# Delta rule: the running inverse of the triangles' substitution in PSUM, and PSUM's banks dealt anew for the projections

## The chip, the cores and the metric

One core of a Trainium2 chip runs the whole program as one launch. The metric is the device time of one execution in microseconds (us); lower is better. The chip's matrix engine is TensorE (PE; its weight loads are listed apart as PEld), the others are VectorE (DVE), ScalarE (ACT), GpSimd (POOL) and SyncE (SP, which here only issues transfers). Each engine works off its own instructions in a fixed order. SBUF is the on-chip memory, and PSUM is the memory that TensorE writes to: here 8 banks, each 128 partitions x 512 fp32 numbers.

## The reference, cut to what matters

Two layers of a hybrid block over 768 tokens (256 of context, 512 latent), model width 1024: attention heads and a gated delta rule (8 heads of width 64, forward and backward) side by side, then a mixture of experts. The delta rule is computed in chunks of 64 tokens, and each chunk needs the inverse of a 64x64 unit lower triangle:

```python
lower = jnp.where(strict, jnp.einsum("bhnid,bhnjd->bhnij", kb, kc) * decay, 0.0)
eye = jnp.eye(CHUNK, dtype=f32)                    # CHUNK = 64
tmat = lax.linalg.triangular_solve(lower + eye, jnp.broadcast_to(eye, lower.shape),
                                   left_side=True, lower=True, unit_diagonal=True)
u = jnp.einsum("bhnij,bhnje->bhnie", tmat, vc * bc)
w = jnp.einsum("bhnij,bhnjd->bhnid", tmat, kb * jnp.exp(gcum)[..., None])
```

## The kernel before, in words

A layer runs: modulation and norm of the input; the **projections** (the stretch that the change touches); attention and the delta rule's 12 steps, interleaved; the output projection; routing and experts. All weights of the projections are split into a high and a low part, so each product is three matmuls (`mm3`, L239): high x high, high x low, low x high.

In the projections the program goes through a written list, `ORDER`, one for each layer. Its items are: `c0` to `c11`, 128 channels each (a weight split, matmuls into the PSUM tile `pt`, an evacuation to `xin` by ScalarE, a five-tap convolution on VectorE, L518); `S`, the gates' scalars; `n256`, `n512`, `n2304`, units of 256 columns of the attention and gate projections (matmuls into `pn`, evacuated by ScalarE to `gev`); and for each of three batches of chunks `i`, `s` and `m`:
- `i` (`delta_intra`): the triangles `u` of a batch, from `kk` (key products, through ScalarE) and `dd` (decays, L790 to L798), and the off-diagonal blocks `uo`. The 32x32 diagonal blocks go to memory (`db`).
- `s` (`delta_subst`): the **substitution**. The 128 partitions hold one 32x32 unit triangle each (`sB`), and `sY` its inverse. 31 steps, two VectorE instructions each: L824 multiplies a column of B with the row of Y that is done into `sT`, and L825 subtracts `sT` from the rows below. Step j works on (31-j)(j+1) numbers of each partition, 31 to 256. Each instruction needs the one before it. At the end `sY` goes to memory (`dy`, L826).
- `m` (`merge_batch`, `delta_merge`): loads `dy` as `yl`, transposes it to `yt`, and joins the 32x32 inverses to 64x64 ones with small matmuls: a pass of L847 into PSUM, a copy `mg` by ScalarE (L848), a pass of L851, a copy into `xm` (L852), twice for each direction d; then `xm` goes to memory (`xad`, L854). There is one `xm` and one `mg`, and one `yl`.

A tile scheduler decides from dependences, priorities and free buffers in which order the items of the list reach each engine, so the items overlap. Behind the list come attention (`kv_stacks` with `kt` L572, `attn_queries` with `qt` L589, the scores `sc` L604) and the delta steps, which load the merged inverses as `lx` (from `xad`) and begin with `pz` (L917).

PSUM is one pool of three kinds of buffers: "a" (`psA`: `pt`, `pn` and others, 512 columns), "c" (`psC`: `kk`, `gb`, `vt`, `kt`, `nps`, a part of the merges), "s" (`psS`, 1024 columns). Before, there are 3 + 3 + one of two banks for the whole program. When the pool is opened again with other numbers, the tiles of the new one wait for the old ones that lie in the same banks.

Of the kernel before, what the change touches and what calls it, by code (L numbers as in the profile page):

```python
# [13 lines left out]
F32 = mybir.dt.float32  # L14
# [3 lines left out]
AF = mybir.ActivationFunctionType  # L18
# [5 lines left out]
P = 128  # L24
# [80 lines left out]
UO = 10  # L105
VR = 1
SB = 2
YB = 2
RQ = 30
FW = ("gpsimd", "gpsimd")  # L110
PSA = (3, 3)
AB = 4
AHEAD = 2
XT = 3
# [7 lines left out]
XM = 1  # L122
DDB = 2
FINP = (8, 9, 10, 11)
MPS = ((0, 1), (0, 1, 2))
ORDER = ("c4 c5 c6 c7 S i0 s0 i1 s1 i2 s2 c0 c1 c2 c3 Q n256 n0 x n512 m0 m1 c8 c10 c11 c9 n2304 m2",
         "c4 c5 c6 c7 S c0 i0 s0 i1 s1 c9 i2 s2 c1 c2 c3 Q n256 n0 x n512 m0 m1 c8 c10 n2304 c11 m2")
WP = 3
# [8 lines left out]
PAIRS = ((0, 1), (2, 5), (3, 4))  # L137
# [7 lines left out]
class Model:  # L145
    def __init__(self, ctx, tc, t):
        self.tc, self.nc, self.t = tc, tc.nc, t
        self.cp = ctx.enter_context(tc.tile_pool(name="const", bufs=1, side=L))
        self.pst = ctx.enter_context(ExitStack())
        self.psum(*PSA)  # L150
        self.dr = ctx.enter_context(tc.tile_pool(name="dr", bufs=1, space=DRAM))
# [48 lines left out]

    def psS(self, name):
        return self.ps.tile([P, 1024], F32, tag="s", bufs=self.ns, name=name)

    def rsq(self, pool, a, name, newton=False):

# [606 lines left out]
    def delta_subst(self, b, db, dy, pool):  # L812

        nc = self.nc
        B = pool.tile([P, 32, 32], F32, tag="sB", bufs=SB, name="sB")
        self.q("ild").dma_start(B, db.rearrange("h q j i -> (h q) j i"))
        Y = pool.tile([P, 32, 32], F32, tag="sY", bufs=YB, name="sY")
        nc.gpsimd.memset(Y, 0.0)
        nc.gpsimd.memset(Y.rearrange("p a b -> p (a b)")[:, 0:1024:33], 1.0)
        for j in range(31):  # L820
            m, w = 31 - j, j + 1
            T = pool.tile([P, 256], F32, tag="sT%d" % (b % ST), bufs=1, name="sT")
            T3 = T[:, :m * w].rearrange("p (a b) -> p a b", a=m)
            nc.vector.tensor_tensor(T3, B[:, j, j + 1:32][:, :, None].to_broadcast([P, m, w]), Y[:, j, 0:w][:, None, :].to_broadcast([P, m, w]), op=OP.mult)  # L824
            nc.vector.tensor_tensor(Y[:, j + 1:32, 0:w], Y[:, j + 1:32, 0:w], T3, op=OP.subtract)  # L825
        self.q("iy").dma_start(dy.rearrange("h q r c -> (h q) r c"), Y)  # L826

    def delta_merge(self, tts, d, dy, us, xad, ps, pool):

# [168 lines left out]
                n = 4 * (2 * d + j)  # L998
                self.delta_intra(tt, d, kk[j], sc, us[tt, d], xad, db[:, n:n + 4], pool)

    def merge_batch(self, i, b, us, xad, dy, pool):
        ps = self.psS("mg") if b in MPS[i] else None
        for d in range(2):
            self.delta_merge(PAIRS[b], d, dy[:, 8 * d:8 * d + 8], us, xad, ps[:, 512 * d:512 * d + 512] if ps is not None else self.psC("mg"), pool)


    def gate(self, mp, ps, n, dst):
# [515 lines left out]
    def layer(self, i, xsrc, rows, done, xstack, mod):  # L1523

        nc, tc, t = self.nc, self.tc, self.t
# [8 lines left out]
        vk, xad, qkd = dr("vk", [NT, P, 2, 512]), dr("xad", [NT, 2, P, 2, 512]), dr("qkd", [NT, P, 512])  # L1534
        db = [dr("db%d_" % b, [NH, 16, 32, 32]) for b in range(3)]
        dy = [dr("dy%d_" % b, [NH, 16, 32, 32]) for b in range(3)]
# [7 lines left out]
        with self.pool("hp", B) as hp:  # L1544
            with self.pool("pj", B) as wp:
                mp.update(self.rope_params(i, wp))
                first = []
                with self.pool("nm", B) as pool:
                    start = lambda: first.extend(self.wnat(i, 2560, 288, wp))
                    hh, hl = self.norm_first(rows, start, pool, hp) if i == 0 else self.norm_mix(i, rows, start, mod, pool, hp)  # L1550
                done()
                mid = left.enter_context(self.pool("mid", A))
                ba = scl.tile([P, NT, 32], F32, name="ba", tag="ba")
                dT = [mid.tile([P, 3088], F32, name="dT%d" % j, tag="dT%d" % j).rearrange("p (a b) -> p a b", a=4) for j in range(2)]

                def nat_unit(c0, n, pool):
                    ws = first if c0 == 2560 else self.wnat(i, c0, n, wp)
                    g = pool.tile([P, NT * UNIT], F32, tag="gev", bufs=GV, name="gev").rearrange("p (t n) -> p t n", t=NT)

                    def ev(tt, ps):  # L1560
                        if c0 < 768:
                            nc.scalar.activation(g[:, tt], ps[:, :UNIT], AF.Copy)  # L1562
                        elif need(tt):
                            self.gate(mp, ps, UNIT, g[:, tt])
                        if n > UNIT:
                            nc.scalar.activation(ba[:, tt, :], ps[:, UNIT:UNIT + 32], AF.Copy)

                    f0 = 0 if c0 in (512, 2560) else t0
                    self.proj_nat(hh, hl, ws, n, range(f0, NT), ev)
                    if c0 < 512:  # L1570
                        self.qk_unit(mp, 0, g, 4, t0, pool)
                        self.q("qg").dma_start(qd[:, t0:, c0:c0 + UNIT], g[:, t0:])
                    elif c0 == 512:
                        self.qk_unit(mp, 1, g, 2, 0, pool)
                        self.q("qg").dma_start(qd[:, :, c0:c0 + UNIT], g)
                    else:
                        self.q("qg").dma_start(gd[:, t0:, c0 - 2304:c0 - 2304 + UNIT], g[:, t0:])

                def conv(f, dst, pool):
                    return self.proj_conv(i, hh, hl, self.wpart(i, 0, 8, 768 + f * P, P, wp), mp["cw"], f, dst, pool)  # L1580

                def key_conv(f, ss, pool):
                    x = dT[f // 4][:, f % 4, :]
                    self.squares(f, x, ss, conv(f, x, pool))
                    if f >= 4:
                        self.token_rows(x, None, vk[:, :, 1, (f - 4) * P:(f - 3) * P], pool)

                def value_conv(f, pool):
                    v = pool.tile([P, NT * UNIT], F32, tag="gev", bufs=GV, name="vf")[:, :772]
                    conv(f, v, pool)  # L1590
                    self.token_rows(v, sc["nk"][:, :, 2 * f - 16:2 * f - 14], vk[:, :, 0, (f - 8) * P:(f - 7) * P], pool)

                with self.pool("pp", B) as pool, self.pool("q1", A) as p1:
                    nat_unit(2560, 288, pool)

                    def query_norms():
                        sc["fq"] = scl.tile([P, NT, NH], F32, name="fq", tag="fq")
                        nc.vector.tensor_scalar(sc["fq"], self.inv_norm(ss, p1)[1], HD ** -0.5, None, op0=OP.mult)

                    us = {}  # L1600
                    for op in ORDER[i].split():
                        kind, arg = op[0], op[1:]
                        if kind == "S":
                            sc = self.delta_scalars(mp, ba, ss, scl, p1)
                        elif kind == "Q":
                            query_norms()
                        elif kind == "c":
                            f = int(arg)
                            if f in (0, 4):
                                ss = self.psS("ss")  # L1610
                            value_conv(f, pool) if f >= 8 else key_conv(f, ss, pool)
                        elif kind == "i":
                            self.intra_batch(int(arg), us, dT, sc, xad, db[int(arg)], p1)
                        elif kind == "s":
                            self.delta_subst(int(arg), db[int(arg)], dy[int(arg)], p1)
                        elif kind == "m":
                            self.merge_batch(i, int(arg), us, xad, dy[int(arg)], p1)
                        elif kind == "x":
                            for tt in range(t0, NT):
                                self.q("qk").dma_start(qkd[tt], self.delta_kk(tt, 0, dT, p1))  # L1620
                        elif kind == "n":
                            nat_unit(int(arg), UNIT, pool)
        o = left.enter_context(self.pool("oo", A)).tile([P, NT, 512], F32, name="o", tag="o")
        wrp = left.enter_context(self.pool("wr", A))
        raws = []
        with self.pool("at", B) as pool:
            st = self.kv_stacks(qd, pool)
            work = ([(pr, 0, 2, 2) for pr in range(4)] if not last else []) + [(pr, 2, 4, 6) for pr in range(4)]
# [161 lines left out]
```

## Time and profile before

| | |
|---|---|
| time, 3 runs | median 2094.74 us (2092.64 to 2094.93) |
| the profiled execution | 2092.51 us, of which the profile's span is 2090.7 us |
| mean granted clock of TensorE | 0.902 of full speed |
| busy: PE / DVE / ACT / POOL | 1763.9 us (84%) / 1460.2 (70%) / 1016.6 (49%) / 868.6 (42%) |
| projections of layer 0 | about 59 to 341 us of the span |
| projections of layer 1 | about 1145 to 1421 us |

The two stretches of projections are 27% of the span. "Busy" is the sum of an engine's instruction times; an engine can be waiting while it counts as busy, where an instruction is held up inside.

### The profile page before, as it was taken

What the parts mean: (1) busy time and instruction counts of PE and PEld (TensorE: products, weight loads), DVE (VectorE), ACT (ScalarE), POOL (GpSimd) and SP (SyncE); (2) the same over time, 40 slices, a digit from 0 to 9 for tenths busy, and PEclk for the clock granted to TensorE, in tenths of its full rate; (3) what the DMA queues carried; (4) which work ended last, traced back from release to release, by engine and by line L of the source; (5) the groups of instructions that cost most, each with busy time, mean ns of one, the idle gap of its engine ahead of it and who ended that gap; (6) DMA issues with size and microseconds to landing.
All of it is one profiled execution on the core that took longest, in us unless ns stands there. A gap on an engine that the chain in (4) does not pass through costs nothing. (4 is left out here: it accounts for less than half of the span.)

```text
span 2090.7 us, 35600 instructions
## 1 busy us (share of the span) xinstructions
PE 1763.9 (84%) x13835; PEld 1382.1 (66%) x13835; DVE 1460.2 (70%) x2472; ACT 1016.6 (49%) x1595; POOL 868.6 (42%) x915
## 2 busy tenths in 40 slices
PE   6998798978877879999996987776898577999994
PEld 4887687766656746666665866675676465777773
DVE  4469996567673668887874579992678465787774
ACT  3444344665541246565554543343566225666663
POOL 4456653234354423343226466650234443334321
PEclk9999897799998979999997998875899788999997
DMA  9222445798645389998853323445983558988872
GB/s 283 74 71 82 129 119 166 218 259 246 205 125 144 147 327 336 332 322 301 324 161 119 97 73 97 131 130 158 282 233 83 148 214 315 346 334 330 328 295 102
DMA packets 227687, 427.81 MB, mean 205 GB/s; under 512 B 83720, under 2 KB 157180, under 8 KB 202939
## 3 DMA queue, kind: packets, MB, share of 16 engines
q1 hardware_dynamic: 171547, 329.09, 47.1%
q0 software_dynamic: 33536, 72.59, 12.2%
q10 hardware_dynamic: 22432, 23.81, 3.3%
q8 instruction: 111, 1.82, 0.4%
q14 instruction: 61, 0.50, 0.1%
HBM read 386.82 MB, written 84.67 MB: 226 GB/s over the span
## 5 line engine op out<-in xcount | busy, mean ns | idle before, releaser
L1418 POOL DMA_INDIRECT yd<-ey,idx x64 | 114.2, 1784 | 425.3 <-DMA yd<-ey,idx 151.8
L1364 PE MATMUL pab<-w,xt 128*128 128x512 f32 x512 | 230.3, 592 | 0.0
L1332 ACT ACTIVATE w2h<-w 128x2048 fp32r<-128x2048 f32 x64 | 122.7, 1917 | 134.5 <-PE py L1406 83.3
L1333 DVE TENSOR_TENSOR w2l<-w,w2h 128x2048 fp32r<-128x2048 f32 x64 | 146.8, 2294 | 53.5 <-ACT w2h L1332 52.9
L1333 DVE TENSOR_TENSOR w13l<-w,w13h 128x2048 fp32r<-128x2048 f32 x64 | 146.5, 2288 | 28.9 <-ACT w13h L1332 28.9
L1364 PEld LDWEIGHTS pab<-w,xt 128*128 128x128 f32 x512 | 93.0, 191 | 92.0 <-issue 91.8
L489 POOL TENSOR_TENSOR wlo<-wraw,whi 128x1024 fp32r<-128x1024 f32 (+1 forms) x44 | 111.1, 2529 | 93.1 <-ACT whi L488 93.1
L239 PE MATMUL pn<-whi,hh 128*128 128x256 f32 (+1 forms) x432 | 134.6, 314 | 16.3 <-ACT gev L1562 12.5
L239 PE MATMUL po<-woh,m 128*128 128x512 f32 x320 | 114.1, 434 | 30.7 <-ACT woh L1069 14.5
L239 PE MATMUL pn<-whi,hl 128*128 128x256 f32 (+1 forms) x432 | 135.3, 316 | 2.0 <-DVE hl L350 1.7
L239 PE MATMUL pn<-wlo,hh 128*128 128x256 f32 (+1 forms) x432 | 132.4, 308 | 1.2 <-POOL wlo L489 1.2
L1332 ACT ACTIVATE w13h<-w 128x2048 fp32r<-128x2048 f32 x64 | 121.8, 1902 | 6.4 <-DMA w<-w 4.1
L239 PE MATMUL pt<-hh,wlo 128*128 128x512 f32 (+1 forms) x352 | 124.2, 353 | 0.0
L239 PE MATMUL pt<-hh,whi 128*128 128x512 f32 (+1 forms) x352 | 122.9, 349 | 0.0
L239 PE MATMUL pt<-hl,whi 128*128 128x512 f32 (+1 forms) x352 | 122.2, 347 | 0.0
L1406 PE MATMUL py<-w2h,gh 128*128 128x512 f32 x256 | 109.1, 426 | 4.6 <-DVE ey L1413 4.4
L1337 POOL DMA_INDIRECT xe<-h2d,idx x64 | 85.9, 1343 | 61.2 <-issue 22.9
L518 DVE SCALAR_TENSOR_TENSOR dT<-xin,cw,dT 128x772 f32<-128x772 f32 x64 | 80.1, 1252 | 43.3 <-ACT dT L516 41.5
L1406 PE MATMUL py<-w2h,gl 128*128 128x512 f32 x256 | 103.1, 403 | 7.8 <-DVE gl L1385 7.8
L1413 DVE TENSOR_TENSOR ey<-py,eg 128x1024 f32<-128x1024 f32 x64 | 78.2, 1222 | 44.1 <-PE py L1406 37.8
L239 PEld LDWEIGHTS pn<-whi,hh 128*128 128x128 f32 x432 | 90.6, 211 | 23.2 <-ACT gev L1562 13.5
L1348 PEld LDWEIGHTS xt<-cst,xe 128*128 128x128 f32 x512 | 68.3, 192 | 55.1 <-issue 29.8
(401 smaller groups left out, 5124.4 us busy)
## 6 DMA issues: line engine op xcount, KB each, us to landing
w<-w SPq DMA_DIRECT2D x192, 1024.0 KB, 9.8
araw<-ada_w POOLq DMA_DIRECT2D x40, 1024.0 KB, 6.8
wraw<-w_in SPq DMA_DIRECT2D x40, 512.0 KB, 4.1
lk<-vk SPq DMA_DIRECT2D x48, 256.0 KB, 7.2
lx<-xad SPq DMA_DIRECT2D x40, 256.0 KB, 10.0
araw<-ada_w SPq DMA_DIRECT2D x8, 1024.0 KB, 10.9
wr<-w_out SPq DMA_DIRECT2D x8, 1024.0 KB, 13.4
vk<-vr ACTq DMA_DIRECT2D x16, 384.0 KB, 3.7
```

Of the source, the lines that this page charges most:

```text
L239: self.nc.tensor.matmul(ps, a(k), b(k), start=(first and n == 0), stop=(last and n == 3 * nk - 1))
L489: getattr(nc, eng).tensor_tensor(lo, raw, hi, op=OP.subtract)
L518: nc.vector.scalar_tensor_tensor(dst, xin[:, tap:tap + 772], cw[:, tap, f:f + 1], dst, op0=OP.mult, op1=OP.add)
L1332: self.pin(nc.scalar.activation(hi, src, AF.Copy))
L1333: self.pin(nc.vector.tensor_tensor(lo, src, hi, op=OP.subtract))
L1337: self.pin(self.nc.gpsimd.indirect_dma_start(out=xe, out_offset=None, in_=h2d, in_offset=bass.IndirectOffsetOnAxis(ap=idx, axis=0), bounds ...
L1348: pin(nc.tensor.transpose(ps[:, k * P:(k + 1) * P], xe.rearrange("p (q k) -> p k q", k=8)[:, 4 * q + k, :], self.ident))
L1364: self.pin(self.nc.tensor.matmul(out, xt[:, k, :], w13[:, :, KS + k, :], start=False, stop=(k == 3)))
L1406: pin(self.nc.tensor.matmul(py[:, n * 512:(n + 1) * 512], a[:, j, :], b[:, c], start=(j + m == 0), stop=(j == 1 and m == 2)))
L1413: pin(nc.vector.tensor_tensor(y, py, gates, op=OP.mult))
L1418: self.pin(self.nc.gpsimd.indirect_dma_start(out=yd, out_offset=bass.IndirectOffsetOnAxis(ap=idx, axis=0), in_=y, in_offset=None, bounds_c ...
```

## The change

The inverse Y of a substitution moves from SBUF (`sY`) to PSUM: to the one "s" buffer, as tile `sP`. The two GpSimd fills of `sY` (L818, L819) go; ScalarE now fills `sP` with zeros (a Copy with scale 0, 128x1024) and VectorE sets the diagonal. The 31 steps are the same instructions on the same shapes, with Y in PSUM in place of SBUF. At the end ScalarE copies `sP` to `sY` in SBUF (now one buffer, before two), and `sY` goes to memory as before. Since `sP` has one buffer, a substitution can't begin before the one ahead of it has been copied out.

For the room, PSUM has two layouts. During the projections "a" has 2 banks in place of 3, "c" has 3, "s" one of two banks, and a new kind "q" (`psQ`) has one bank: it takes the merges (`mg`) and the squares' sums (`ss`), which were in "s" and "c". The layout is switched behind the norm and back ahead of attention, twice in each layer.

```diff
-YB = 2
+YB = 1
...
-PSA = (3, 3)
+PSA, PSB = (3, 3), (2, 3)
...
-MPS = ((0, 1), (0, 1, 2))
...
+    def psQ(self, name):
+        return self.ps.tile([P, 512], F32, tag="q", bufs=1, name=name)
...
         self.q("ild").dma_start(B, db.rearrange("h q j i -> (h q) j i"))
-        Y = pool.tile([P, 32, 32], F32, tag="sY", bufs=YB, name="sY")
-        nc.gpsimd.memset(Y, 0.0)
-        nc.gpsimd.memset(Y.rearrange("p a b -> p (a b)")[:, 0:1024:33], 1.0)
+        ps = self.psS("sP")
+        Y = ps.rearrange("p (a b) -> p a b", a=32)
+        nc.scalar.activation(ps, self.cst[:, :1024], AF.Copy, scale=0.0)
+        nc.vector.memset(ps[:, 0:1024:33], 1.0)
         for j in range(31):
...
-        self.q("iy").dma_start(dy.rearrange("h q r c -> (h q) r c"), Y)
+        res = pool.tile([P, 32, 32], F32, tag="sY", bufs=YB, name="sY")
+        nc.scalar.activation(res, Y, AF.Copy)
+        self.q("iy").dma_start(dy.rearrange("h q r c -> (h q) r c"), res)
...
-    def merge_batch(self, i, b, us, xad, dy, pool):
-        ps = self.psS("mg") if b in MPS[i] else None
+    def merge_batch(self, b, us, xad, dy, pool):
         for d in range(2):
-            self.delta_merge(PAIRS[b], d, dy[:, 8 * d:8 * d + 8], us, xad, ps[:, 512 * d:512 * d + 512] if ps is not None else self.psC("mg"), pool)
+            self.delta_merge(PAIRS[b], d, dy[:, 8 * d:8 * d + 8], us, xad, self.psQ("mg"), pool)
...
                 done()
+                self.psum(*PSB)
...
-                                ss = self.psS("ss")
+                                ss = self.psQ("ss")
...
+        self.psum(*PSA)
         with self.pool("at", B) as pool:
```

The lines behind the edits move down by 2 to 5 in the changed kernel (L239 is L241 there, L824 and L825 are L827 and L828). In the rows below a number behind a name tells tiles of one name apart.

**Place 1: TensorE at the end of the norm, layer 1.** `nps` are the norm's transposes, `pn` the matmuls of the first unit of the projections. Before, they alternate:

```order
L343 MATMUL nps<-cst,x_11014 128x128
L239 MATMUL pn<-whi,hl 128x288
L239 MATMUL pn<-whi,hh 128x288
L239 MATMUL pn<-wlo,hh 128x288
L239 MATMUL pn<-whi,hl 128x288
L343 MATMUL nps<-cst,x_11012 128x128
L343 MATMUL nps<-cst,x_11014 128x128
L239 MATMUL pn<-whi,hh 128x288
```

Now the unit stands behind all of the norm:

```order
L345 MATMUL nps<-cst,x_11028 128x128
L345 MATMUL nps<-cst,x_11030 128x128
L345 MATMUL nps<-cst,x_11028 128x128
L345 MATMUL nps<-cst,x_11030 128x128
L241 MATMUL pn<-whi,hh 128x288
L241 MATMUL pn<-wlo,hh 128x288
L241 MATMUL pn<-whi,hl 128x288
```

Of the unit's 144 matmuls, 72 (layer 0) and 108 (layer 1) stood ahead of the norm's last transpose; now none does, in either layer.

**Place 2: VectorE at the turn from substitution 0 to 1, layer 0.** Before, the two are interleaved, with other work between (`ud` is of `delta_intra`):

```order
L824 TENSOR_TENSOR sT_1308<-sB_1264,sY_1266 128x252
L824 TENSOR_TENSOR sT_1486<-sB_1481,sY_1483 128x31
L825 TENSOR_TENSOR sY_1266<-sY_1266,sT_1308 128x18x14
L825 TENSOR_TENSOR sY_1483<-sY_1483,sT_1486 128x31
L824 TENSOR_TENSOR sT_1311<-sB_1264,sY_1266 128x255
L805 SCALAR_TENSOR_TENSOR ud_1636<-u_1632,cst_63,ud_1636 128x256
L824 TENSOR_TENSOR sT_1489<-sB_1481,sY_1483 128x60
L825 TENSOR_TENSOR sY_1266<-sY_1266,sT_1311 128x17x15
```

Now they follow each other, with the last steps of one, three instructions of an attention unit, and the first step of the next:

```order
L827 TENSOR_TENSOR sT_1363<-sB_1268,sP_1270 128x31
L828 TENSOR_TENSOR sP_1270<-sP_1270,sT_1363 128x31
L538 TENSOR_REDUCE qss_2537<-qsq_2535 128x8
L540 TENSOR_SCALAR qss_2537<-qss_2537 128x8
L822 MEMSET sP_1489 128x32
L542 TENSOR_TENSOR gev_2352<-gev_2352,qr_2540 128x512
L827 TENSOR_TENSOR sT_1492<-sB_1487,sP_1489 128x31
```

In layer 1 the MEMSET stands directly behind the last step at both turns. Over the program's 372 such instructions, 121 stood directly behind the one of the same substitution that they need; now 231 do.

**Place 3: TensorE at the end of the projections, layer 0.** `pn` is the last unit, `mg` the last merges, `kt`, `qt` and `sc` attention. Before, attention stands among the merges:

```order
L239 MATMUL pn<-whi,hl 128x256
L847 MATMUL mg<-yt,uo 32x32 x32
L851 MATMUL mg<-yl,mg 32x32 x16
L572 MATMUL kt<-cst,xl 128x128 x6
L589 MATMUL qt<-cst,ql 128x128 x2
L851 MATMUL mg<-yl,mg 32x32 x16
L604 MATMUL sc<-ka,qs 128x256
```

Now all merges come first:

```order
L241 MATMUL pn<-whi,hl 128x256
L852 MATMUL mg<-yt,uo 32x32 x16
L856 MATMUL mg<-yl,mg 32x32 x32
L852 MATMUL mg<-yl,uo 32x32 x32
L856 MATMUL mg<-yt,mg 32x32 x32
L852 MATMUL mg<-yt,uo 32x32 x32
L856 MATMUL mg<-yl,mg 32x32 x32
L574 MATMUL kt<-cst,xl 128x128 x6
L591 MATMUL qt<-cst,ql 128x128 x2
L606 MATMUL sc<-ka,qs 128x256
L606 MATMUL sc<-kb,qs 128x256
L922 MATMUL pz<-lk,lx 64x64
```

In layer 1 `kt` and `qt` stood ahead of the last batch's merges, and now stand behind them.

## Rows read from the trace of the kernel before

**Rows 1.** Windows: busy PE, PEld, DVE, ACT, POOL; clock; DMA share; GB/s

```profile
165.00:342.00 177.00, 150.82 (x1487) 134.59 (x1487) 167.32 (x330) 69.51 (x134) 99.10 (x90) 0.91 0.38 106
342.00:393.00 51.00, 41.94 (x459) 35.71 (x459) 20.38 (x56) 34.09 (x82) 10.25 (x13) 0.53 0.59 180
1260.00:1421.50 161.50, 121.35 (x1180) 106.57 (x1180) 150.01 (x319) 61.18 (x118) 99.46 (x81) 0.82 0.45 128
```

**Rows 2.** Timeline, ends of the projections: start, length, instruction, [idle before <-releaser]

```profile
338.44 0.19 DVE L825 TENSOR_TENSOR sY<-sY,sT 128x31 f32<-128x31 f32 x1
341.41 0.28 PE L239 MATMUL pn<-whi,hl 128*128 128x256 f32 x1
...
393.27 0.47 PE L917 MATMUL pz<-lk,lx 64*64 64x64 f32 x2
...
1421.03 0.19 DVE L825 TENSOR_TENSOR sY<-sY,sT 128x31 f32<-128x31 f32 x1
...
1451.78 1.91 PE L851 MATMUL mg<-yl,mg 32*32 32x32 f32 x32 [0.74 <-ACT xm L852]
...
1461.24 0.45 PE L917 MATMUL pz<-lk,lx 64*64 64x64 f32 x2 [0.23 <-DMA lx<-xad]
```

**Rows 3.** Windows, VectorE busy in L824 alone, then in L825

```profile
165.00:342.00 177.00, 44.95 (x93) 0.91 0.38 106
1260.00:1421.50 161.50, 42.46 (x93) 0.82 0.45 128
...
165.00:342.00 177.00, 42.67 (x93) 0.91 0.38 106
1260.00:1421.50 161.50, 38.71 (x93) 0.82 0.45 128
```

**Rows 4.** Timeline of VectorE, two neighbouring steps in layer 1

```profile
1396.53 0.42 DVE L824 TENSOR_TENSOR sT<-sB,sY 128x252 f32<-128x252 f32 x1
1396.98 0.42 DVE L825 TENSOR_TENSOR sY<-sY,sT 128x252 f32<-128x252 f32 x1
```

**Rows 5.** Timeline of VectorE and of GpSimd, the same moment in layer 0

```profile
303.02 0.41 DVE L824 TENSOR_TENSOR sT<-sB,sY 128x252 f32<-128x252 f32 x1
303.34 1.02 DVE L518 SCALAR_TENSOR_TENSOR vf<-xin,cw,vf 128x772 f32<-128x772 f32 x1
...
305.54 2.62 DVE L824 TENSOR_TENSOR sT<-sB,sY 128x255 f32<-128x255 f32 x1
...
304.74 3.14 POOL L489 TENSOR_TENSOR wlo<-wraw,whi 128x1024 fp32r<-128x1024 f32 x1 [6.36 <-ACT whi L488]
```

**Rows 6.** Instructions of two lines: ns min/median/max; first and last start; shapes

```profile
L793 DVE TENSOR_TENSOR dd<-gb,gcum x24: 643/678/693, 135.2 to 1321.6; 128x512 f32<-128x512 f32 x24
L798 DVE TENSOR_TENSOR u<-kks,dd x24: 676/685/2884, 148.3 to 1331.9; 128x512 f32<-128x512 f32 x24
```

**Rows 7.** The same view: two more lines

```profile
L326 ACT ACTIVATE sq<-x x12: 1009/1027/1029, 17.4 to 1126.6; 128x1024 f32<-128x1024 f32 x12
L347 DVE TENSOR_SCALAR nT<-nps,fm x18: 527/536/545, 25.0 to 59.3; 128x256 f32<-128x256 f32 x18
```

**Rows 8.** Timeline of TensorE behind layer 1's norm; `pn` back to back

```profile
1146.18 0.30 PE L239 MATMUL pn<-whi,hh 128*128 128x288 f32 x1
1146.31 0.30 PE L239 MATMUL pn<-wlo,hh 128*128 128x288 f32 x1
```

**Rows 9.** What TensorE waited for, 60 to 342 us: total, times, longest

```profile
PE kk L778 <- ACT kks L781: 7.5, 3, 5.0
PE kk L778 <- DVE dd L793: 7.3, 2, 3.7
PE pn L239 <- ACT gev L1562: 5.9, 1, 5.9
PE pn L239 <- ACT ba L1566: 3.1, 1, 3.1
```

**Rows 10.** The same for ScalarE

```profile
ACT uo L802 <- DVE u L798: 30.0, 9, 5.1
```

More of the change, by code (lines that the diff above doesn't have):

```diff
@@ L1616, in layer @@
                         elif kind == "m":
-                            self.merge_batch(i, int(arg), us, xad, dy[int(arg)], p1)
+                            self.merge_batch(int(arg), us, xad, dy[int(arg)], p1)
                         elif kind == "x":
```

## Prediction

> **What bounds the kernel now.** I first cut the span into stretches and read each engine's busy time, then looked at where the two stretches of projections end, then at the substitution's own instructions. In [rows 1] the reader is to see that VectorE is the engine that sets the second half of the projections: in layer 0, 167.3 of 177 us busy against 150.8 of TensorE, so TensorE stands idle for 26 us; in layer 1, 150.0 of 161.5 against 121.4, with 40 us idle and a granted clock of 0.82. Behind it comes a stretch with little work at half clock (0.53). The chain that matters is in [rows 2]: the last subtraction of substitution 2 ends at 338.6 and 1421.2 us, then come the merges, and the delta steps begin (`pz`) at 393.3 and 1461.2. In layer 0 TensorE's last projection ends 3 us after the substitution, so both engines end together there; in layer 1 the substitution alone is last.
>
> Now the substitution itself. By [rows 3] its 186 instructions in a layer take 44.95 + 42.67 = 87.6 us in layer 0 and 42.46 + 38.71 = 81.2 in layer 1, half of VectorE's time. What would they take undisturbed? The shortest form, 31 numbers, takes 0.19 us [rows 2], and 252 numbers take 0.42 [rows 4]: 1.04 ns for a number, and 0.16 fixed. The 31 steps have 5456 numbers, twice: 62 x 0.15 + 10912 x 0.00104 = 20.7 us for a substitution, 62 for a layer. So 25 us in layer 0 and 19 in layer 1 are excess. Where it comes from is in [rows 5]: a 255-number multiplication takes 2.62 us, and GpSimd begins `wlo`, from SBUF to SBUF, in the same stretch; it lasts 3.14. [Rows 6] show the same on a pair of lines with equal shape: L798, both operands in SBUF, ranges from 676 to 2884 ns; L793, one operand in PSUM, never takes more than 693 in 24 times. In PSUM, Y makes both instructions of a step like L793.
>
> **The change part by part.**
>
> The collisions: −25 and −19 us of VectorE, if [rows 6] carry over. They hold for a PSUM operand that is read. L827 only reads one; L828 also writes to PSUM, and no row shows a VectorE instruction that does. Bounds: the dearest PSUM operand is L347, 0.536 us for 256 numbers [rows 7] against 0.42, so +0.12 on the 186 writes, 22 us in all; below, L793's 678 against L798's 685, nothing. I take nothing, since L793 is the nearest row: same operation, same engine, a two-operand form.
>
> The steps follow each other closer. 110 more instructions stand directly behind the one that they need (231 against 121). Such a neighbour begins 0.03 us after the end of the other (1396.98 − 1396.53 = 0.45 at a length of 0.42 [rows 4]); an independent one begins 0.09 before it (303.34 against 303.02 + 0.41 [rows 5]). 110 x 0.12 = 13 us, 6.5 a layer.
>
> The turns between substitutions. The one `sP` is copied out by ScalarE, zeroed by ScalarE, and given its diagonal, before the next can begin. A Square of 128x1024 into PSUM takes 1.03 us [rows 7]; I take that for fill and for copy, with 0.2 for the MEMSET and some 0.3 for the hand-overs: 2.5 us. Where other VectorE work stands between, it is covered: by the order one turn of layer 0 and none of layer 1, so 2.5 and 5 us. The first fill and the GpSimd fills that go cost and bring nothing: no one waits for them.
>
> So VectorE's part is −25 + 6.5 + 2.5 = −16 in layer 0, and −19 + 6.5 + 5 = −7 in layer 1, where `kt` and `qt` also go behind the merges, and take their VectorE work out of the stretch; I count −2 for that, what is left when they are done later at a better clock.
>
> The switch of the layout. TensorE no longer puts the first unit into the gaps of the norm. 72 and 108 matmuls that lay beside the norm now follow it, at 0.13 us each by [rows 8] (I count 0.136, with the gaps between groups): 10 and 15 us. Against it: the norm ends a little sooner without them, 2 to 3 us, and in layer 0 the 3.1 us wait for `ba` [rows 9] no longer comes in the same way. I take +5 and +12. The bounds are 0 (if VectorE's chain behind it had room) and 25 in all.
>
> Two banks "a" in place of three. A tile has 24 matmuls, 2.9 us at 256 columns (0.136 x 256/288 = 0.12). TensorE can be one tile less ahead of ScalarE, so a late evacuation costs up to a tile. Below: the two places where three banks ran out already, `gev` 5.9 and `ba` 3.1 us [rows 9], 6 us in all. Above: ScalarE itself stands 9 times behind VectorE's `u` [rows 10], up to 5.1 us, and each would cost a tile, 26 us. I take 6, since TensorE waits for an evacuation only in those two rows; most of ScalarE's idle time is not on a `pt`.
>
> The end of the projections, layer 0. Substitution 2 ends at 338.6 − 16 + 5 = 328. TensorE: of its 26 idle us some 14 were waits for `kks` and `dd` (7.5 + 7.3 [rows 9]), which follow VectorE; 341.7 − 14 + 5 + 3 = 336. The merges then run with nothing between, from the end of the last unit: in layer 1 the like of it took from 1421.2 to 1453.7, 32.5 us [rows 2], with passes of 1.91 + 0.74. So 368; `xad` and its loads 7 us, as from 1453.7 to 1461.2: `pz` at 375, 18 sooner. But the attention that stood among the merges is now behind them. In the 51 us from 342 TensorE was busy for 41.9 at a clock of 0.53 [rows 1]; some 12 passes of the merges, 1.91 each [rows 2], are 23 of it, and the other 19 are attention, 10 us at full clock, less what fits in the 7 us of loads: +8. Layer 0: −10, with bounds −18 (the attention hides) and 0.
>
> Layer 1: +12 −7 −2, one more ScalarE copy ahead of `dy`, +1, and 3 for the banks' lower bound, which leaves +5 after 2 us of the switch's loss have gone into waits for `dd`. The sum: −10 + 5 = −5 us. Against the profiled execution, 2092.5: 2087.5; the median lies 2.2 higher, so I forecast **2089.7**, say 2090.
>
> **The rivals.**
>
> Bigger gain: TensorE follows VectorE fully. For: 40 idle us and a clock of 0.82 in layer 1 [rows 1]; at 0.95 its 121 us would be 105. With layer 0 at its bound, −18, and layer 1 at −8, −26: 2069. Against: the idle time has several releasers, and the switch takes place ahead of it.
>
> Nothing to see: VectorE's gain is real but the switch's lower cost in TensorE's order, 10 + 15 us, takes all of it. It needs only 5 us more than I count: 2095.
>
> Two banks decide, and the kernel gets slower. The place is the stretch of `c` items with `i` between, where ScalarE waits for `u` and can't empty `pt`. The price is 2.9 us each time; from 4 such tiles beyond the two that I count the change loses, and with all nine it is 20 us more: 2110. For: 30 us of such waits [rows 10]. Against: TensorE's list of waits has hardly a `pt` in it.
>
> PSUM itself costs: each instruction with Y in PSUM is dearer by a fixed time, as L347 is by 0.12 us [rows 7]. On the 186 writes that is 22 us, of which some 18 reach the end: 2108; on all 372, 2130. [...]
>
> **How the numbers follow.** The forecast's own range is 2080 to 2099: layer 0's bounds, and 5 either way for switch and banks. Chances: the forecast 0.42, the bigger gain 0.15, nothing to see 0.12, two banks 0.17, PSUM itself 0.09, something else 0.05 (slower). The range from 2068 to 2110 takes in the bigger gain and the two banks and leaves out the far end of PSUM itself and of the rest. A run of this kernel can tell some 0.2%, 4.2 us, from no change: faster is below 2090.5, slower above 2098.9. Of the forecast's 0.42, 0.25 lies below and 0.15 within, 0.02 above; so faster 0.42, same 0.27, slower 0.31.
>
> **What would show it.** Right: L827 and L828 in two windows at 62 to 65 us a layer with no single one above 0.6 us, whatever GpSimd does; neighbours 0.03 us apart; a gap of 2 to 3 us at the turns of layer 1; `pn` beginning behind the last `nps`; `pz` near 375 us in layer 0 and near 1466 in layer 1 less what layer 0 gave. Wrong: L828's shortest form at 0.25 us or more (PSUM itself), TensorE waits for `xin` or `gev` of 15 us and more in a layer (two banks), or long instructions still among L827 and L828, which would put their cause elsewhere than at the shared reads.

## The result, and the profile after

The changed kernel takes **2122.3 us** (median, 2122.09 to 2132.77 in 4 runs) against 2094.84 of the kernel before in the same comparison: ratio 1.0143, 95% interval 1.0117 to 1.0169. It is slower by 27.5 us; the forecast was 2090 (2068 to 2110).

The substitution did what was forecast. Its two lines in the changed kernel, as instructions of a line (ns min/median/max, first and last start):

```profile
L827 DVE TENSOR_TENSOR sT<-sB,sP x186: 173/353/422, 190.7 to 1453.4; 128x31 f32<-128x31 f32 x12, 128x60 f32<-128x60 f32 x12, 128x87 f32<-128x87 f32 x12, 128x112 f32<-128x112 f32 x12
L828 DVE TENSOR_TENSOR sP<-sP,sT x186: 180/366/432, 192.0 to 1453.6; 128x31 f32<-128x31 f32 x12, 128x60 f32<-128x60 f32 x12, 128x87 f32<-128x87 f32 x12, 128x112 f32<-128x112 f32 x12
```

The windows of L827, then of L828, as [rows 3]:

```profile
165.00:342.00 177.00, 30.80 (x93) 0.91 0.45 131
1300.00:1460.00 160.00, 30.96 (x93) 0.77 0.48 139
...
165.00:342.00 177.00, 32.05 (x93) 0.91 0.45 131
1300.00:1460.00 160.00, 31.99 (x93) 0.77 0.48 139
```

No instruction is above 0.432 us, where before one of 2.62 stood beside GpSimd's `wlo` [rows 5]. A layer's 186 instructions take 62.9 us, against 87.6 and 81.2 [rows 3]. The ends of the stretches, on the timelines of VectorE and TensorE, as [rows 2]; the last three rows are the end of attention in layer 0 and layer 1's first `pz`:

```profile
337.42 0.20 DVE L828 TENSOR_TENSOR sP<-sP,sT 128x31 f32<-128x31 f32 x1
...
328.08 0.28 PE L241 MATMUL pn<-whi,hl 128*128 128x256 f32 x1
370.20 1.91 PE L856 MATMUL mg<-yl,mg 32*32 32x32 f32 x32 [0.74 <-ACT xm L857]
372.05 1.86 PE L574 MATMUL kt<-cst,xl 128*128 128x128 f32 x6
378.62 0.45 PE L922 MATMUL pz<-lk,lx 64*64 64x64 f32 x2 [0.48 <-DMA lx<-xad]
...
609.22 0.33 PE L903 MATMUL pq<-S,dT 64*64 64x64 f32 x4
635.24 0.39 PE L647 MATMUL pv<-pl,vs 128*128 128x512 f32 x1
...
1487.27 0.32 PE L922 MATMUL pz<-lk,lx 64*64 64x64 f32 x2
```

Up to layer 0's first `pz` the change is ahead: 378.6 against 393.3 [rows 2]. The lead is not where the forecast had it: the last subtraction ends at 337.6, only 1 us sooner than before, but TensorE's last projection ends at 328.4, 13 us sooner, and the last merge is done 34.5 us behind the substitution, where it was 47 before (at 386.0).

But attention's last value (`pv`) comes at 635.2, 26 us behind the last delta step (`pq`, 609.2). In the kernel before the last values start at 599.7, among the last delta steps (its last `pq` starts at 601.5). Values of layer 0 before (two halves), then after:

```profile
L645 PE MATMUL pv<-ph,vs x64: 280/398/628, 365.3 to 599.5; 128*128 128x512 f32 x48, 128*128 128x256 f32 x16
L645 PE MATMUL pv<-pl,vs x64: 279/394/628, 366.1 to 599.7; 128*128 128x512 f32 x48, 128*128 128x256 f32 x16
```

```profile
L647 PE MATMUL pv<-ph,vs x64: 279/393/793, 385.2 to 635.0; 128*128 128x512 f32 x48, 128*128 128x256 f32 x16
L647 PE MATMUL pv<-pl,vs x64: 278/398/795, 386.4 to 635.2; 128*128 128x512 f32 x48, 128*128 128x256 f32 x16
```

So from `pz` to the last value layer 0 takes 257 us in place of 207. Layer 1's first instruction on TensorE (`cw`) comes at 1132.1 in place of 1104.2: 27.9 of the 29.8 us that lie between the two profiled executions. From there to its first `pz` layer 1 takes 355.2 us against 357.0.

What attention's tail looks like, on TensorE's timeline of the changed kernel and then ScalarE's:

```profile
616.39 1.54 PE L628 MATMUL ptr<-cst,pp 128*128 128x128 f32 x6 [3.39 <-ACT pp L620]
622.17 1.54 PE L628 MATMUL ptr<-cst,pp 128*128 128x128 f32 x6 [4.24 <-ACT pp L620]
625.90 0.79 PE L647 MATMUL pv<-ph,vs 128*128 128x512 f32 x1 [2.19 <-ACT ph L639]
```

```profile
618.36 2.94 ACT L1073 ACTIVATE woh<-wr 128x1024 fp32r<-128x1024 f32 x3
621.20 0.92 ACT L620 ACTIVATE pp<-pp,sm 128x768 f32<-128x768 f32 x1
622.02 2.94 ACT L1073 ACTIVATE woh<-wr 128x1024 fp32r<-128x1024 f32 x3
```

With no delta step left to fill the gaps, TensorE waits 2 to 4 us at links of the chain score, maximum, exponential, scale (`pp`), transpose (`ptr`), `ph`, value; and on ScalarE the links queue behind the output projection's weight splits `woh`, three at a time, 2.9 us.

### The profile page after: what moved, and what is told of

It reads as the page before. It is cut to its first block, busy times and chain, and to the rows that moved or that the text cites. A ratio compares the mean times of both kernels' runs of the same rounds, so it can differ in the third digit from the quotient of the medians.

```text
span 2120.5 us, 35611 instructions
## 1 busy us (share of the span) xinstructions
PE 1777.8 (84%) x13835; PEld 1384.9 (65%) x13835; DVE 1421.8 (67%) x2478; ACT 1028.1 (48%) x1607; POOL 840.2 (40%) x903
## 5 line engine op out<-in xcount | busy, mean ns | idle before, releaser
L1422 POOL DMA_INDIRECT yd<-ey,idx x64 | 120.2, 1878 | 417.4 <-DMA yd<-ey,idx 161.0
L241 PE MATMUL pn<-whi,hh 128*128 128x256 f32 (+1 forms) x432 | 132.3, 307 | 5.1 <-ACT gev L1567 3.0
L241 PE MATMUL po<-woh,m 128*128 128x512 f32 x320 | 111.0, 424 | 27.9 <-ACT m L1045 15.6
L241 PE MATMUL pn<-wlo,hh 128*128 128x256 f32 (+1 forms) x432 | 130.7, 303 | 3.1 <-POOL wlo L491 3.1
L241 PE MATMUL pn<-whi,hl 128*128 128x256 f32 (+1 forms) x432 | 130.5, 302 | 0.0
L241 PE MATMUL pt<-hh,wlo 128*128 128x512 f32 (+1 forms) x352 | 123.4, 351 | 0.0
L241 PE MATMUL pt<-hh,whi 128*128 128x512 f32 (+1 forms) x352 | 122.0, 347 | 0.0
L241 PE MATMUL pt<-hl,whi 128*128 128x512 f32 (+1 forms) x352 | 121.7, 346 | 0.0
L1352 PEld LDWEIGHTS xt<-cst,xe 128*128 128x128 f32 x512 | 68.2, 192 | 58.5 <-issue 29.8
L1366 PE MATMUL pab<-w13h,xth 128*128 128x512 f32 x256 | 103.0, 403 | 0.5 <-ACT xth L1354 0.5
```

The costliest lines, as they stand in the source:

```text
L241: self.nc.tensor.matmul(ps, a(k), b(k), start=(first and n == 0), stop=(last and n == 3 * nk - 1))
L1352: pin(nc.tensor.transpose(ps[:, k * P:(k + 1) * P], xe.rearrange("p (q k) -> p k q", k=8)[:, 4 * q + k, :], self.ident))
L1366: self.pin(self.nc.tensor.matmul(out, a[:, k, :], b[:, :, k, :], start=(k + m == 0), stop=False))
L1422: self.pin(self.nc.gpsimd.indirect_dma_start(out=yd, out_offset=bass.IndirectOffsetOnAxis(ap=idx, axis=0), in_=y, in_offset=None, bounds_c ...
```

## The experiments

Each was timed beside the kernel before, whose median was 2094 to 2096 us in each of the comparisons. The marks below are from the profiled execution: the start of the first `pz` and the end of the last `pv` of layer 0, the start of layer 1 (`cw`), and the time from there to layer 1's first `pz`.

| kernel | pz, layer 0 | last pv, layer 0 | layer 1 starts | to its pz | time, median | ratio to before (95%) |
|---|---|---|---|---|---|---|
| before | 393.3 | 600.1 | 1104.2 | 357.0 | 2094.8 | 1 |
| changed | 378.6 | 635.6 | 1132.1 | 355.2 | 2122.3 | 1.0143 (1.0117 to 1.0169) |
| e1 gate | 383.2 | 631.8 | 1118.4 | 358.0 | 2116.3 | 1.0108 (1.0063 to 1.0152) |
| e2 late | 383.3 | 613.8 | 1109.4 | 374.1 | 2119.8 | 1.0124 (1.0080 to 1.0169) |
| e3 layout | 388.5 | 651.9 | 1140.1 | 363.5 | 2146.7 | 1.0267 (1.0213 to 1.0321) |
| e4 sub | 402.8 | 660.7 | 1153.8 | 360.1 | 2148.2 | 1.0257 (1.0212 to 1.0301) |
| e5 l0 | 387.6 | 626.0 | 1120.0 | 357.3 | 2105.1 | 1.0055 (1.0031 to 1.0079) |
| e6 l0q | 378.2 | 616.8 | 1110.5 | 357.3 | 2111.2 | 1.0096 (1.0064 to 1.0127) |
| e7 early | 377.1 | 618.1 | 1108.3 | 350.6 | 2094.0 | 0.9997 (0.9971 to 1.0023) |
| e8 norm | 396.9 | 624.0 | 1127.5 | 371.3 | 2131.0 | 1.0182 (1.0138 to 1.0225) |
| e9 norm, order | 397.0 | 606.0 | 1106.8 | 375.5 | 2111.8 | 1.0102 (1.0066 to 1.0138) |
| e10 after, order | 403.8 | 609.2 | 1110.7 | 358.5 | 2106.8 | 1.0073 (1.0038 to 1.0108) |
| e11 best | 381.3 | 601.3 | 1101.9 | 354.8 | 2092.3 | 0.9989 (0.9968 to 1.0010) |
| e12 best, Y in SBUF | 399.9 | 621.2 | 1120.9 | 365.6 | 2118.4 | 1.0130 (1.0103 to 1.0157) |

Each mark is of a single execution, and it scatters. In layer 0, e2 and e5 have the same instructions, on each engine in the same order but for a few neighbours that changed places; yet their last values come 12 us apart, and layer 1 starts at 1109.4 in one and at 1120.0 in the other. (e2's profile is of a run of 2111.9 us, where the median is 2119.8; e5's of one of 2112.0, where it is 2105.1.) So some 10 us between two marks show nothing by themselves; the times have to agree. The values of layer 0 in e2, then in e5:

```profile
L647 PE MATMUL pv<-ph,vs x64: 279/396/797, 352.0 to 612.7; 128*128 128x512 f32 x48, 128*128 128x256 f32 x16
L647 PE MATMUL pv<-ph,vs x64: 281/398/795, 357.0 to 625.0; 128*128 128x512 f32 x48, 128*128 128x256 f32 x16
```

**First round: where is the loss?** Theory A: the switch ahead of attention. Theory B: the projections, by two banks or by PSUM as such.

e1, on the kernel before:

```diff
         raws = []
+        self.psum(*PSA)
         with self.pool("at", B) as pool:
```

> The kernel before, with PSUM's pool opened anew (same 3, 3 and one) ahead of attention and nothing else. Theory A (the switch back ahead of attention is the loss: attention waits for the last merge and has no head start over the delta steps): in layer 0 two scores instead of 24 ahead of step 0, an attention tail of 20 to 35 us behind the last delta step, 2115 to 2130 us in all; the substitution is untouched. Theory B (the loss is in the projections: two banks, or PSUM as such): no switch of numbers, Y in SBUF, so 2090 to 2100.

Theory A holds: with Y and the layout untouched, opening the pool anew puts all merges ahead of `kt` and attention's tail behind the delta steps, and costs 20.7 us, of which 14 show at the start of layer 1. The first and last `pz` and the values of layer 0 in e1:

```profile
L917 PE MATMUL pz<-lk,lx x384: 217/218/364, 383.2 to 596.8; 64*64 64x64 f32 x192
L645 PE MATMUL pv<-ph,vs x64: 277/397/796, 390.2 to 631.2; 128*128 128x512 f32 x48, 128*128 128x256 f32 x16
```

The scheduler's order of attention and delta steps changes with it, so e1 alone does not part the late start from the order.

e2, on the changed kernel:

```diff
-        self.psum(*PSA)
         with self.pool("at", B) as pool:
...
             for g in (fill, ada):
                 for _ in g:
                     pass
             self.pins(False)
+            self.psum(*PSA)
```

> The changed kernel, with the switch back to the old layout moved from ahead of attention to behind it (attention then has two banks of kind a). Theory A: 22 scores ahead of step 0 again, no tail of 20 us or more, 28 to 36 us less than the changed kernel: 2086 to 2096. Theory B: attention with two banks is no better and the projections are as they were: 2115 to 2125 or more.

A miss: 2119.8. Layer 0 got back 22.7 us (1109.4 against 1132.1), but layer 1 lost 19: its first `pz` comes 374.1 us after its start. There 32 scores in place of 4 now stand ahead of the first `pz`, between the last merges on TensorE and ScalarE, and the merges are what the delta steps wait for: from the end of the substitution to `pz` 44.1 us in place of 33.5. The other 8 us lie ahead of the substitution's end and were not followed. One place, two signs: layer 0 has attention as its end, layer 1 the delta steps.

e3, the changed kernel with the old `delta_subst` and `YB = 2`:

> The changed kernel with the inverse Y back in SBUF (two buffers, filled by GpSimd), the new layout and both switches kept. If the collisions are what Y in PSUM takes away and VectorE sets the end of layer 0's projections: single steps of 2 us and more come back, L824 and L825's places take 80 to 88 us a layer instead of 62, the last merge of layer 0 comes 10 to 16 us later, 2132 to 2150 in all. If Y in PSUM brings nothing that reaches the end: 2118 to 2126.

Inside: 2146.7, 24 us above the changed kernel. Y in PSUM is worth that much in these layouts, the order that the scheduler makes of each included. e4, the kernel before with the new `delta_subst`, and:

```diff
-MPS = ((0, 1), (0, 1, 2))
+MPS = ((), ())
...
-                                ss = self.psS("ss")
+                                ss = self.psC("ss")
```

> The kernel before, with Y in PSUM (the one s buffer) and no new layout: 3 banks a, 3 banks c, no switch; the merges and the sums of squares go to kind c. Theory A: the gain of the substitution (16 us of VectorE in layer 0, 7 in layer 1) without norm's and attention's loss; 12 scores ahead of step 0, half the head start of before: 2075 to 2092. Theory B, PSUM as such: 2100 or more.

It did not test what it should: 2148.2. With merges and sums in kind "c" the last unit of layer 0 ends at 367.2 (341.7 before), and TensorE waits 17.1 us for `gx` in nine places, where 1.4 was the sum of before. The old layout has no room for Y in this way; why `gx` came late was not followed further.

**Second round: parts of the way back.** e5 is e2 in layer 0 alone (`if last:` ahead of the first switch, `if not last:` ahead of the second).

> The changed kernel, with the switch back to the old layout moved behind attention in layer 0 alone; in layer 1 it stays ahead of attention. Theory A2 (layer 0 ends with attention, a long chain that needs its head start; layer 1 ends with the delta steps, which the last merges must reach early, so the same switch helps there): layer 0 as in the run with both switches moved, layer 1 as in the changed kernel: 2097 to 2106. If layer 1's loss in that run came from two banks in attention as such, layer 0 should lose as much and this run stays at 2110 to 2122.

Inside: 2105.1, 17 us below the changed kernel. Against e2, which differs in layer 1 alone, it is 15 us less: there the switch ahead of attention is the better one. e6 gives attention's values the bank "q" in layer 0:

```diff
-        u.pv = self.psA("pv")
+        u.pv = self.psQ("pv") if "pv" in self.qt else self.psA("pv")
```

> As the run before, and in layer 0 the values of attention (pv) go to the one bank of kind q, so that attention has three banks again. If two banks make attention slower in layer 0 (269 us from first score to last value against 244 before), 5 to 15 us less than the run before: 2085 to 2100. If only the head start counts (16 scores ahead of step 0 here, 22 there), the same or up to 5 us more.

A miss for the third bank: 2111.2, 6 us above e5. With 16 scores ahead of step 0 in place of 22 the order changed too, so what the bank alone is worth is not shown. e7 is e6 with `self.psum(*PSB)` at the head of the layer in place of behind the norm; e8 is the kernel before with `self.psum(*PSA)` behind the norm, and nothing else.

> As the run before, and the new layout is opened at the head of the layer, ahead of the norm, so that the first unit's matmuls go beside the norm again (48 and 96 of 144 ahead of its last transpose; 72 and 108 in the kernel before, none in the changed one). If the switch behind the norm costs what the first traces show at the start of the projections (6 us in layer 0, 10 in layer 1) and it reaches the end: 2072 to 2090. If it is swallowed by waits later on: as the run before, within 5 us.

> The kernel before, with PSUM's pool opened anew (same 3, 3 and one) behind the norm and nothing else. The projections begin 5 to 6 us later in layer 0 and 10 later in layer 1. If that reaches the end: 2100 to 2112. If waits later on swallow it: 2092 to 2098.

Both miss their ranges. e7 is 17 us below e6: the switch behind the norm does cost, but the kernel only comes level with before. By the marks, `pz` gains 1.1 us in layer 0 and 6.7 in layer 1; where the rest lies was not followed. And e8 was the surprise: 37 us for a pool opened anew, of which layer 0 has 23 at layer 1's start, though its `pz` is only 3.6 late and the same 24 scores stand ahead of it; another 14 lie in layer 1 ahead of its `pz`. What differs in layer 0 is behind `pz`: from attention's first `kt` on, the order on TensorE is that of before for 420 instructions, to about 5 us behind the first `pz`; then the scheduler interleaves the same instructions in another way. In none of the kernels so far did layer 0 take less than 227 us from `pz` to the last `pv`; before, 207.

**Third round: the order itself.** Theory C: the order of attention and delta steps, which the scheduler derives anew after any shift, is what runs longer. In e9 to e12 the instructions of that stretch were tied on each engine to the order of the kernel before, which is written out as a table (`RANK`; the lines around it are left out):

```diff
+        last = {}
+        for j in struct.unpack("<%dH" % (len(raw) // 2), raw):
+            x = ins[k + j]
+            e = x.engine.name
+            if e in last:
+                self.tc.add_manual_dep(x, last[e], mybir.DependencyInfo(mybir.DependencyClass.NoSync, mybir.DependencyReason.DATA), reason="order")
+            last[e] = x.name
```

e9 is e8, e10 the changed kernel, each with the order of before in layer 0.

> The kernel of the run e8 (before, pool opened anew behind the norm), with the 2414 instructions of layer 0's attention and delta steps put by hand into the very order on each engine that they have in the kernel before. Theory C (a shift ahead makes the scheduler interleave attention and delta steps in another order, and that order is what runs longer): from the first pz to the last pv 205 to 213 us in layer 0 instead of 227, araw waits of 13 to 16 us instead of 23; 2108 to 2117 in all. If the order is not it (transfers, clock): 2124 to 2134.

> The changed kernel, with the same instructions of layer 0 in the order of the kernel before among themselves; attention still waits for the merges, so the delta steps now wait for its 24 scores. Theory C: from kt (372) some 250 us to the last pv as before, which is 620 to 624 instead of 636: 2104 to 2114 in all. If only the late start counts: 2118 to 2126.

Both times are inside, and e10's last value comes sooner than expected. e9 is 19 us below e8, and the stretch from `pz` to the last value takes 209 us. What e9 is still above before, 18 us, lies in layer 1, whose order was left to the scheduler: its `pz` comes 375.5 us after its start, 357.0 before. The windows of that stretch, e8 and then e9 (columns as in [rows 1]):

```profile
397.00:624.00 227.00, 185.97 (x2683) 138.59 (x2683) 146.18 (x311) 119.01 (x230) 89.58 (x96) 0.87 0.71 203
```

```profile
397.00:606.00 209.00, 172.58 (x2614) 130.83 (x2613) 142.76 (x306) 115.92 (x227) 86.69 (x93) 0.92 0.77 221
```

In the worse order TensorE idles 41.0 us against 36.4 and is busy 13.4 us longer, at a granted clock of 0.87 against 0.92; 69 more matmuls fall into the stretch, of delta steps that stand behind the last value in the better order. Its waits for `araw` in layer 0, e8 and e9:

```profile
PE aps L265 <- DMA araw<-ada_w: 23.4, 7, 7.6
```

```profile
PE aps L281 <- DMA araw<-ada_w: 12.8, 3, 7.6
```

These waits alone don't make the difference: in e2 and e5, of one order, they are 15.5 and 21.0 us. That the order costs is shown by the times; by which of its waits it costs is not.

e10 parts the late start from the order. Its delta steps begin 25 us later than those of the changed kernel (403.8), since 24 scores must go first, and yet attention ends 26 us sooner (609.2):

```profile
L663 PE MATMUL pv<-pl,vs x64: 279/396/793, 382.8 to 608.8; 128*128 128x512 f32 x48, 128*128 128x256 f32 x16
L938 PE MATMUL pz<-lk,lx x384: 218/218/366, 403.8 to 605.5; 64*64 64x64 f32 x192
```

e11 joins what helped: Y in PSUM, the new layout opened ahead of the norm, back behind attention in layer 0 and ahead of it in layer 1, the order of before in both layers. e12 is e11 with Y in SBUF.

> Y in PSUM, the new layout opened ahead of the norm, the switch back behind attention in layer 0 and ahead of it in layer 1, and both layers' attention and delta steps in the order of the kernel before (attention of layer 0 with two banks). Theory C: layer 0 gains the 14 to 16 us at pz and loses 0 to 10 of it to two banks, layer 1 gains some 5 against e7: 2068 to 2086. If the order doesn't matter: as e7, 2090 to 2098.

> As e11, with Y back in SBUF: layouts, switches and the order of attention are the same, so the difference is Y's place alone. By the forecast's steps VectorE is 16 us longer in layer 0 and 7 to 13 in layer 1, of which most reaches pz: 15 to 25 us more than e11. If Y in PSUM brings nothing that reaches the end: within 4 us of e11.

e11 is 30 us below the changed kernel and level with the kernel before (0.9968 to 1.0010), above what was expected. e12 is 26 us above e11, a little over the range: that is Y's place, with the order of the projections that the scheduler makes for it; 18.6 us show at `pz` in layer 0 and 10.8 in layer 1. It is not the substitution that ends sooner in e11: its last subtraction ends at 339.9, in e12 at 339.0. TensorE's last projection does (324.6 against 346.0), and with it the last merge (372.4 against 387.2): in 165 to 342 us VectorE gets through 344 instructions in e11 and 329 in e12. Which of them TensorE had waited for was not followed. In e12 the subtractions again reach 2.63 us:

```profile
L843 DVE TENSOR_TENSOR sY<-sY,sT x186: 184/374/2634, 185.6 to 1432.4; 128x31 f32<-128x31 f32 x12, 128x60 f32<-128x60 f32 x12, 128x87 f32<-128x87 f32 x12, 128x112 f32<-128x112 f32 x12
```

What holds e11 back in layer 0 is probably attention on two banks: 220 us from `pz` to the last value in place of 207. TensorE waits there 22 times for `pl`, which is computed from the transposes in these banks; `ptr` and `qt` don't read `pl`, so what they wait for is a bank. In the kernel before TensorE waited for `pl` twice, 6.2 us in all. And a score waits for the "s" buffer, which `sP` holds until it is copied out. From 340 to 660 us:

```profile
PE ptr L644 <- DVE pl L656: 11.1, 10, 2.1
PE pv L663 <- DVE pl L656: 6.6, 7, 2.0
PE qt L607 <- DVE pl L656: 5.4, 5, 1.9
PE sc L622 <- ACT sY L846: 5.1, 1, 5.1
```

Of the 13 us between the two stretches, TensorE's idle time is 6 (40.1 against 34.5); the rest is busy time at a granted clock of 0.90 against 0.93. A layout that keeps three banks for attention and doesn't wait for the merges was not tried on the chip with that order, so the banks' share is not shown.

## Why the prediction was wrong

The step that failed is the one on the end of layer 0's projections: "attention that stood among the merges is now behind them ... 10 us at full clock, less what fits in the 7 us of loads: +8". It priced displaced attention by TensorE's work, 8 us. Measured, `pz` came 14.7 us sooner and layer 1 began 27.9 later: behind `pz` layer 0 lost 42.6 us, and from `pz` to the last value it took 50 more. The forecast for the layer was −10 in all. The runs show two causes in its place:

- Attention is a chain of short links, and the changed kernel starts it behind the merges with 2 scores ahead of the delta steps in place of 24; its tail then runs alone. The switch back holds it until the last merge (e1: 20.7 us on the kernel before with nothing else changed; e5: 17 us back from the changed kernel).
- The price hangs on the order that the scheduler then makes of attention and delta steps. With the order of before, the same gate costs 15 us less (e10), although the delta steps start later. I had read the order only up to the first `pz`. Why one order runs longer than another stays open.

The other steps:

- **Collisions.** Right: −25 and −19 us forecast, 62.9 us left in each layer, where 62 were forecast (with the fixed 0.16 us that the prediction had found, where its sum took 0.15, it would have been 64). The shortest multiplication takes 173 ns with Y in PSUM and 177 in SBUF, the shortest subtraction, which also writes Y, 180 and 176. That is 4 ns at the shortest, 0.7 us on the 186 writes, where the rival "PSUM itself" had 22: it is refuted. The long ones go with GpSimd: by the start and end times in the two traces, all 63 of the 372 instructions that took longer than 432 ns before overlap an instruction of GpSimd, as do 144 of the other 309; in the changed kernel 211 of the 372 overlap one, and none takes longer than 432 ns (2621 before). With Y back in SBUF they reach 2634 ns again (e12). Why some that overlap are long and others are not isn't shown.
- **Turns.** Right: 2.5 us forecast, 2.2 measured. VectorE in layer 1 between substitutions 0 and 1:

```profile
1372.06 0.20 DVE L828 TENSOR_TENSOR sP<-sP,sT 128x31 f32<-128x31 f32 x1
1374.46 0.09 DVE L822 MEMSET sP<- 128x32 f32 x1 [2.20 <-ACT sP L821]
```

- **The way to pz.** Near, and by luck: layer 0 at 378.6, forecast 375, last merge 372.1, forecast 368. Two errors went against each other. Substitution 2 was to end at 328 and ended at 337.6; TensorE's projections were to end at 336 and ended at 328.4. The three substitutions span 146.9 us in place of 154.2, though their instructions take 25 us less; what else filled the time was not followed.
- **The switch behind the norm.** The sum fits, the places don't: 5 and 12 us were forecast, and e7 is 17 below e6, but by the marks `pz` gains only 1.1 us in layer 0 and 6.7 in layer 1. On the kernel before, the same switch (e8) makes `pz` 3.6 and 14.3 us late. The first unit of the projections ends 5.9 us later than before in layer 0 and 9.7 in layer 1; in layer 0 it scatters from 0.7 to 5.9 over the kernels with this switch.
- **Two banks in the projections.** No cost shows. TensorE's waits for an evacuation in layer 0's projections fell to 1.0 us (`gev`), from 9.0 [rows 9], and in layer 1's they are 2.0 for `gev` and 4.3 for `xin`; the sign for this rival was 15. The rivals that had the kernel slower (2110 for the banks, 2108 and 2130 for PSUM itself) had it so for reasons that the rows refute.

```profile
PE pn L241 <- ACT gev L1567: 1.0, 2, 0.7
```

- **Layer 1.** Forecast +5; measured −1.8 up to `pz` and +2 over the layer, from one execution each.

As a rough sum: Y in PSUM −26 (e12 to e11), the switch behind the norm +17 (e6 to e7), and, as the rest of +27.5, some +36 for the switch back and the order that it led to, of which e10 shows 15 to be layer 0's order. The parts come from different kernels, and e8 shows that even the norm's switch reaches attention's order; that they add up is not shown.

## What to carry to other kernels

Where a scheduler fixes the order of a long interleaved stretch, read that stretch in the order of both kernels, however far it lies from the edit; a pool opened anew ahead of it (e8) made layer 0's attention run 18 to 20 us longer, and its old order took that back (e9). Price displaced work by the chain that it belongs to and by what covers that chain later, not by an engine's busy time. A pool of buffers that is opened anew is a barrier: ask who stands behind it at each place: ahead of attention, the same barrier cost layer 0 of the changed kernel 17 us (e5 took it out) and saved layer 1 15 (e2 took it out as well).

## What the runs showed of the hardware that was not expected

With attention and delta steps in another order, TensorE was granted 0.87 of full speed in place of 0.92 over some 200 us (e8 against e9, one execution each); in e2 and e5, of one order, it was 0.88 and 0.87. VectorE's MEMSET of 32 numbers a partition into PSUM shows as 0.09 us in each of its six rows, ScalarE's fill of 1024 numbers a partition into PSUM as 1.00 to 1.05 in its six, and its copy out as 1.02 to 1.03. VectorE's subtractions in place took 180, 366 and 432 ns in PSUM (shortest, median, longest), and 176, 374 and 2575 in SBUF.
